# Reordering a list of twenty-five emission steps between an output projection and an up projection

## The chip, the cores and the metric

One core of a Trainium2 chip runs the whole program. The metric is the device time of one execution in microseconds (us); the median of several runs is compared.

## The reference

One layer of an encoder is applied to two batches, 512 and 256 positions (768 rows in all), 1024 channels, all in float32:

```
x = layernorm(x)
bg, cg, hc, q, k, v = split(x @ w_in)            # six blocks of 512 columns
y_conv = bg * dwconv3(cg * hc)                   # depthwise, three taps
y_attn = neighbourhood_attention(q, k, v, rpb)   # 8 heads of 64
y = concat(rmsnorm(y_conv), rmsnorm(y_attn))
x = layernorm(ALPHA * x + y @ w_o)               # the stage of this change
gate, val = split(dwconv3(x @ w_up))             # 1024 -> 2 * 2816
x = layernorm(ALPHA * x + (gelu(gate) * val) @ w_down)
```

## The kernel before, in words

The rows lie in six tiles of 128 positions, numbered 0 to 5. Tiles 2a and 2a+1 hold the even and the odd positions of a block of 256, so there are three blocks (a = 0, 1, 2). Every float32 matrix operand is split in a high part (a cast on ScalarE, line 99) and a low part (a subtraction on VectorE or GpSimd, line 100), and a product is three matmuls.

The up projection isn't done on even and odd positions one by one. It works on seven combinations ("roles" 1 to 7) of the even and odd operands and of the weights, so that seven products stand for eight. Buffer AR holds the seven combinations of x as operands: 0 and 1 are the two halves of the even tile, 2 comes from the odd tile alone, and 3, 4, 5, 6 are sums and differences of both. `OPS` (role to operand) is {1: 0, 2: 1, 3: 2, 4: 6, 5: 3, 6: 4, 7: 5}. So roles 1 and 2 need only even tiles; the others need the odd tile too.

The stage of this change stands between the attention half of the output projection (line 801) and the main loop of the up projection. Its pieces, by the letters of the list in the diff:

- `w`t is `wo_conv(t)`: 24 matmuls of 512 columns for tile t (line 822), in two halves; each half is added to the residual on VectorE (line 823). Then the norm of the tile: small VectorE sums (824, 209), a Square with a sum on ScalarE (210), a small VectorE operation (211), a power on GpSimd (212), a small VectorE product (826), and the scaling of the tile on ScalarE (827).
- `e`a is `x_even(a)`: eight TensorE transpositions of tile 2a (line 250), scaled out of PSUM by ScalarE (line 844), and then two operand splits (0 and 1).
- `o`a is `x_odd(a)`: the same for tile 2a+1, where VectorE scales one half (line 842), and then operands 2, 3, 5, 4, 6 in this order, with four VectorE sums or differences (lines 862, 864, 867, 869).
- `p`i prepares the weights of role i for the first pair of channel blocks (adds at lines 170 and 173, splits at 99 and 100).
- `a`i is `step(0, i, columns 0 to 255)`: the part of the first up product of role i that needs only blocks 0 and 1, 12 matmuls (line 180). After roles 1, 7 and 6 ScalarE copies the sum to another bank (lines 957, 963, 966), since a later role goes on from it; lines 943 and 949 fill parts of a bank that aren't summed yet.
- `l`c starts the loads of weights.

The rest of those roles (130 columns, block 2) and everything after is issued by the main loop, on TensorE in the order of the text. In the stage of the change only the transfers that SyncE starts (SP) are held to the order of the text (`tc.manual_schedule(engines={SP.engine})`). For the other engines a planner places the instructions ahead of time: the order of the text is their rank when several are ready by its own reckoning, and one that is ready earlier may stand earlier. The order on each engine is then fixed. The tiles `zt`, into which the transposed halves go, have seven buffers; PSUM has eight banks.

In this text "a1" means the 12 matmuls of `a1`, "tile 5's transpositions" the eight of `o2`, and so on; "piece i" is the 130-column rest of role i of the first pair. The steps that wait for each other around the change are these lines:

```python
V.scalar_tensor_tensor(o, q, ra[:, 0, t:t + 1], o, op0=OP.mult, op1=OP.add, accum_out=mv[:, n:n + 1])  # 823
A.activation(acc[t], acc[t], AF.Identity, bias=mv[:, 2:3], scale=mv[:, 3:4])                           # 827
q = transposed(bank("tr"), kn(acc[t])[:, 4 * c:4 * c + 4])                                             # x_tr
A.copy(role(c, 2)[:, n], role(c, 1)[:, n])                                                             # 957
```

Of the kernel before, what the change touches and what calls it, by code (L numbers as in the profile page):

```python
# [48 lines left out]
def encoder_kernel(ctx, tc, x, lnp, wv, wproj, wo_a, wo_c, wup, wdn, chan, rpb, mask, ident, out):  # L49
# [4 lines left out]
    def pool(name, **kw):  # L54
        g = tc.tile_pool(name=name, bufs=1, reuse_waits="tile", **kw)
        p = g.__enter__()
        return p, lambda: g.__exit__(None, None, None)
# [11 lines left out]
    def f(ap):  # L69
        return ap.bitcast(F32)  # L70
# [112 lines left out]
    a1, a1_close = pool("a1", side="right")  # L183
# [215 lines left out]
    a2, a2_close = pool("a2", side="right")  # L399
# [596 lines left out]
          "p": lambda i: pairs[0].prep(i), "a": lambda i: step(0, i, slice(0, Z0))}  # L996
    V.memset(f(AR[:, :, :, :, Z0:Z0 + 1]), 0.0)
    V.memset(f(AR[:, :, :, :, Z1:Z1 + 1]), 0.0)
    for z in "l0 l1 w0 p1 w1 e0 w2 o0 p7 w3 e1 p6 w4 o1 p2 w5 e2 p4 a1 a7 o2 a6 a2 a4 p5".split():
        EM[z[0]](int(z[1]))  # L1000
    lp_close()
    bp_close()
# [5 lines left out]
    for c in range(NC):  # L1008
        z = [(c, i) for i in (1, 7, 6, 2, 4, 5)]
# [233 lines left out]
```

## Time and profile before

| what | value |
|---|---|
| median of 3 runs | 864.44 us (864.15 to 867.42) |
| the profiled execution: its time, its span | 869.34 us, 867.6 us |
| TensorE busy, share of the span | 94% |
| VectorE busy | 79% |
| ScalarE busy | 57% |
| GpSimd busy | 26% |
| mean granted TensorE clock | 0.983 |

The span is the time from the first to the last instruction on the chip; the execution's own time is 1.74 us longer. The profiled execution was slower than the median of the runs by 4.9 us. Busy shares are averages over stages of different kinds.

### The profile page before, as it was taken

The numbers are of one execution on the slowest core, as the hardware profiler recorded it, in microseconds if no ns is written. First come the engines' busy times: TensorE is split into PE (matmuls) and PEld (weight loads), VectorE is DVE, ScalarE is ACT, GpSimd is POOL, SyncE is SP. The second block draws the span as 40 slices with busy tenths as digits, with TensorE's granted clock in tenths as the row PEclk, the third lists the DMA queues.
The fourth block names the chain that finished last, engine by engine and source line by source line (L and its number), as shares of the span: only waits on it lengthen the run. The fifth ranks groups of instructions, "written<-read, shape, count | busy, mean of one in ns | idle before, by whom it ended". The sixth has DMA issues, their size and how long they took to land.

```text
span 867.6 us, 13319 instructions
## 1 busy us (share of the span) xinstructions
PE 817.1 (94%) x4391; PEld 753.9 (87%) x4391; DVE 688.6 (79%) x1335; ACT 492.3 (57%) x1020; POOL 228.8 (26%) x286
## 2 busy tenths in 40 slices
PE   4899999979999999899999999999999889999995
PEld 3678999969898777899999999999999868888884
DVE  6997758867777667788888888888988699975675
ACT  4755656755676448765656555555556458445060
POOL 3555251354402431221433242232301000000101
PEclk9999999989999999899999999999999989999998
DMA  8688778776726750486998998899732399893361
GB/s 326 207 215 215 174 183 203 165 168 141 193 89 214 251 123 13 97 237 176 253 243 238 233 257 232 236 237 228 215 111 82 105 363 337 281 317 104 107 243 73
DMA packets 86421, 171.02 MB, mean 197 GB/s; under 512 B 12848, under 2 KB 26400, under 8 KB 86000
## 3 DMA queue, kind: packets, MB, share of 16 engines
q1 hardware_dynamic: 59552, 110.87, 39.5%
q0 software_dynamic: 25216, 54.74, 28.7%
q10 hardware_dynamic: 1584, 4.56, 1.3%
q8 instruction: 34, 0.56, 0.3%
q14 instruction: 35, 0.29, 0.1%
HBM read 142.70 MB, written 50.48 MB: 223 GB/s over the span
## 4 chain that ended last, share of the span: by engine, by line
PE 74%; DVE 10%; DMA 6%; ACT 5%; issue 3%; POOL 2%; SPq 0%; POOLq 0%; DVEq 0%; ACTq 0%
PE u L180 37%; PE dn L1061 19%; PE r L180 13%; DVE w L100 3%; DMA acc<-xa_d 2%; PE O L680 1%; PE S L623 1%; DVE AR L100 1%; ACT AR L99 1%; DMA vw<-v_d 1%; PE PT L656 1%; DMA br<-in_rpb 1%; DMA gb<-in_lnp 1%; DVE xr L233 1%; ACT sq L210 1%
## 5 line engine op out<-in xcount | busy, mean ns | idle before, releaser
L180 PE MATMUL u<-AR,w 128*128 128x386 f32 (+2 forms) x1908 | 333.5, 336 | 3.5 <-ACT u L957 3.5
L180 PEld LDWEIGHTS u<-AR,w 128*128 128x128 f32 x1908 | 332.2, 190 | 3.9 <-ACT u L957 3.8
L100 DVE TENSOR_TENSOR w<-raw,w 128x512 fp32r<-128x512 f32 x248 | 173.8, 713 | 59.2 <-ACT w L99 58.2
L99 ACT CAST w<-raw 128x512 fp32r<-128x512 f32 x255 | 156.4, 619 | 96.8 <-PE r L180 29.2
L1061 PE MATMUL dn<-w,hs 128*128 128x512 f32 (+1 forms) x714 | 163.6, 391 | 7.0 <-ACT hs L99 4.2
L1061 PEld LDWEIGHTS dn<-w,hs 128*128 128x128 f32 x714 | 132.4, 190 | 37.9 <-ACT hs L99 4.5
L180 PE MATMUL r<-AR,w 128*128 128x384 f32 x840 | 159.9, 342 | 2.4 <-ACT w L99 0.7
L180 PEld LDWEIGHTS r<-AR,w 128*128 128x128 f32 x840 | 146.9, 190 | 3.8 <-ACT w L99 1.0
L364 POOL DMA_DIRECT2D sw_d<-in_wdn x44 | 37.3, 929 | 106.3 <-DMA sw_d<-sw_d 82.5
L887 DVE SCALAR_TENSOR_TENSOR cu<-u,ch,cu 128x385 f32<-128x385 f32 (+1 forms) x88 | 52.1, 613 | 11.3 <-ACT cu L892 6.5
L99 ACT CAST hs<-hr 128x386 fp32r<-128x386 f32 x75 | 38.5, 514 | 36.9 <-DMA hr<-h_d 26.6
L100 DVE TENSOR_TENSOR w<-rw,w 128x512 fp32r<-128x512 f32 x70 | 47.1, 686 | 8.3 <-ACT w L99 8.3
L99 ACT CAST w<-rw 128x512 fp32r<-128x512 f32 x70 | 43.3, 621 | 15.8 <-issue 12.0
L887 DVE SCALAR_TENSOR_TENSOR cu<-cu,fwn 128x385 f32<-128x385 f32 (+1 forms) x88 | 48.5, 615 | 0.3 <-ACT cu L892 0.3
L909 POOL DMA_DIRECT2D h_d<-cu x33 | 24.2, 735 | 86.2 <-DVE cu L914 81.4
L1083 POOL TENSOR_TENSOR mv<-mv,expo 128x1 f32<-128x1 f32 x6 | 5.1, 854 | 157.9 <-DVE mv L1084 157.9
L100 DVE TENSOR_TENSOR hs<-hr,hs 128x386 fp32r<-128x386 f32 x75 | 41.0, 555 | 3.5 <-ACT hs L99 3.4
L801 PE MATMUL wo<-w,AR 128*128 128x512 f32 x144 | 34.5, 396 | 1.8 <-DVE acc L807 1.8
L822 PE MATMUL woc<-w,AR 128*128 128x512 f32 x144 | 34.7, 397 | 0.0
L801 PEld LDWEIGHTS wo<-w,AR 128*128 128x128 f32 x144 | 26.7, 188 | 8.5 <-DVE acc L807 2.6
L822 PEld LDWEIGHTS woc<-w,AR 128*128 128x128 f32 x144 | 26.8, 188 | 6.1
L303 PE MATMUL vp<-w,AR 128*128 128x512 f32 x108 | 29.2, 417 | 2.7 <-DVE AR L100 1.2
(193 smaller groups left out, 1078.8 us busy)
## 6 DMA issues: line engine op xcount, KB each, us to landing
raw<-in_wup SPq DMA_DIRECT2D x60, 256.0 KB, 6.5
hr<-h_d SPq DMA_DIRECT2D x75, 193.0 KB, 4.7
raw<-in_wproj SPq DMA_DIRECT2D x50, 256.0 KB, 5.4
rw<-in_wup SPq DMA_DIRECT2D x50, 256.0 KB, 6.8
sw_d<-in_wdn POOLq DMA_DIRECT2D x44, 256.0 KB, 9.5
raw<-sw_d SPq DMA_DIRECT2D x44, 256.0 KB, 4.7
raw<-in_wdn SPq DMA_DIRECT2D x33, 256.0 KB, 4.7
h_d<-ho POOLq DMA_DIRECT2D x11, 579.0 KB, 4.1
```

Of the source, the lines that this page charges most:

```text
L99: A.copy(hi, src)
L100: eng.tensor_sub(lo, src, f(hi))
L180: PE.matmul(q, w[:, g, k], AR[:, OPS[i], h, k, n], start=start and m == 0, stop=stop and m == 11, skip_group_check=True)
L210: A.activation(scratch, src, AF.Square, bias=mv[:, 0:1], accum_out=mv[:, 2:3])
L233: V.scalar_tensor_tensor(dst[n], dst[n], mv[:, 3:4], b[n], op0=OP.mult, op1=OP.add)
L303: PE.matmul(q, x_part(t, c)[:, h, k], wvo[4 * c + k][:, g], start=c + m + k == 0, stop=c == 1 and m == 2 and k == 3)
L364: return lambda: G.dma_start(sw_d[j, SW[i]], src, accum_op=OP.add)
L801: PE.matmul(banks[t], yas(h, i, t), wt[k][:, g], start=i == 0 and m == 0, stop=i == 3 and m == 2)
L822: PE.matmul(q, ycs(h, i, t), woc[i][n][:, g], start=i == 0 and m == 0, stop=i == 3 and m == 2)
L887: V.scalar_tensor_tensor(c[:, e, n], u[:, m], w, c[:, e, n], op0=OP.mult, op1=OP.add)
L909: G.dma_start(h_d[j, i:i + n].rearrange("o p n -> p o n"), src)
L1061: PE.matmul(q[:, x], hs[i, j][:, h, cols(a)], wd[i, j][:, g, x], start=i in (1, 7) and j == 0 and m == 0, stop=j == NJ - 1 and m == 2, ski ...
```

## The change

One string is changed: the order in which the steps of this stage are emitted. `w5` moves ahead of `o1` and `p2`; `a1` moves ahead of `e2` and `p4`; `o2` moves from behind `a7` to behind `a2`, ahead of `a4`. No instruction is added or removed.

```diff
     V.memset(f(AR[:, :, :, :, Z0:Z0 + 1]), 0.0)
     V.memset(f(AR[:, :, :, :, Z1:Z1 + 1]), 0.0)
-    for z in "l0 l1 w0 p1 w1 e0 w2 o0 p7 w3 e1 p6 w4 o1 p2 w5 e2 p4 a1 a7 o2 a6 a2 a4 p5".split():
+    for z in "l0 l1 w0 p1 w1 e0 w2 o0 p7 w3 e1 p6 w4 w5 o1 p2 a1 e2 p4 a7 a6 a2 o2 a4 p5".split():
         EM[z[0]](int(z[1]))
```

## Rows read from the trace of the kernel before

**Rows 1.** Page, part 1: busy us (share), instructions

```profile
PE 817.1 (94%) x4391; PEld 753.9 (87%) x4391; DVE 688.6 (79%) x1335; ACT 492.3 (57%) x1020; POOL 228.8 (26%) x286
```

**Rows 2.** Windows by stage: stretch, its length, busy us by engine, granted clock, DMA

```profile
307.50:366.00 58.50, 52.70 (x281) 44.72 (x279) 39.96 (x101) 40.67 (x81) 10.97 (x14) 0.94 0.32 72
366.00:450.00 84.00, 84.00 (x488) 84.00 (x489) 72.67 (x124) 50.97 (x90) 24.88 (x31) 1.00 0.81 218
...
690.00:720.00 30.00, 22.97 (x92) 18.11 (x91) 25.85 (x40) 16.98 (x33) 2.03 (x3) 0.89 0.94 332
```

**Rows 3.** TensorE in order of time: start, us, what [idle before, releaser]

```profile
341.21 1.09 PE L250 MATMUL tr<-idt,acc 128*128 128x128 f32 x8 [1.15 <-ACT acc L827]
342.06 5.83 PE L822 MATMUL woc<-w,AR 128*128 128x512 f32 x24
347.72 1.04 PE L250 MATMUL tr<-idt,acc 128*128 128x128 f32 x8
348.51 1.66 PE L180 MATMUL u<-AR,w 128*128 128x256 f32 x12
...
350.19 1.58 PE L180 MATMUL u<-AR,w 128*128 128x256 f32 x12
355.05 2.50 PE L180 MATMUL u<-AR,w 128*128 128x256 f32 x10 [3.28 <-ACT u L957]
357.35 1.91 PE L250 MATMUL tr<-idt,acc 128*128 128x128 f32 x8
...
359.80 6.00 PE L180 MATMUL u<-AR,w 128*128 128x256 f32 x48
366.00 8.54 PE L180 MATMUL u<-AR,w 128*128 128x130 f32 x60 [0.20 <-ACT u L957]
```

**Rows 4.** Windows of the stage, columns as in rows 2

```profile
341.00:342.00 1.00, 0.79 (x7) 0.79 (x8) 0.50 (x3) 1.00 (x3) 0.00 (x0) 1.00 0.00 0
...
352.00:354.00 2.00, 0.00 (x0) 0.00 (x0) 1.36 (x4) 2.00 (x5) 0.42 (x1) 0.93 0.34 131
...
355.00:356.00 1.00, 0.95 (x4) 0.95 (x5) 0.76 (x2) 0.63 (x1) 1.00 (x3) 0.50 0.00 0
...
360.00:362.00 2.00, 2.00 (x17) 2.00 (x16) 1.97 (x6) 1.58 (x3) 0.00 (x0) 0.86 0.92 166
```

**Rows 5.** ScalarE in order of time

```profile
344.49 1.25 ACT L827 ACTIVATE acc<-acc,mv 128x1024 f32<-128x1024 f32 x1
...
351.04 1.53 ACT L844 ACTIVATE zt<-tr,ch 128x128 f32<-128x128 f32 x4
352.42 0.66 ACT L99 CAST AR<-zt 128x512 fp32r<-128x512 f32 x1
352.93 1.19 ACT L210 ACTIVATE sq<-acc,mv 128x1024 f32<-128x1024 f32 x1
...
354.58 0.41 ACT L957 COPY u<-u 128x256 f32<-128x256 f32 x1
355.37 1.24 ACT L827 ACTIVATE acc<-acc,mv 128x1024 f32<-128x1024 f32 x1 [0.38 <-DVE mv L826]
```

**Rows 6.** VectorE in order of time

```profile
312.08 0.69 DVE L173 TENSOR_TENSOR raw<-raw 128x512 f32<-128x512 f32 x1
...
340.10 0.75 DVE L823 SCALAR_TENSOR_TENSOR acc<-woc,ra,acc 128x512 f32<-128x512 f32 x1 [0.28 <-PE woc L822]
...
349.13 0.69 DVE L100 TENSOR_TENSOR AR<-zt,AR 128x512 fp32r<-128x512 f32 x1
...
350.93 0.75 DVE L823 SCALAR_TENSOR_TENSOR acc<-woc,ra,acc 128x512 f32<-128x512 f32 x1
...
359.29 1.37 DVE L842 TENSOR_SCALAR zt<-tr,ch 128x128 f32<-128x128 f32 x4 [3.41 <-PE tr L250]
...
365.08 1.42 DVE L100 TENSOR_TENSOR AR<-zt,AR 128x512 fp32r<-128x512 f32 x2
```

**Rows 7.** GpSimd in order of time

```profile
351.24 1.18 POOL L100 TENSOR_TENSOR AR<-zt,AR 128x512 fp32r<-128x512 f32 x1 [7.03 <-ACT AR L99]
```

## The prediction

> **What bounds the kernel now.** I read the page first: TensorE is busy for 817.1 of 867.6 us [rows 1], so only what it loses can be won. The windows by stage show where. From 307.5 to 366 it is busy for 52.7 of 58.5 us at a mean clock of 0.94; from 366 to 450 it is busy for 84.00 of 84.00 [rows 2]. So in the up projection nothing but TensorE sets the time, and a microsecond won before 366 is carried on; its loss around 690 [rows 2] lies in the change to the down projection, which begins when the up products end, and moves along with them.
>
> TensorE in order of time shows what is lost near the change [rows 3]: 1.15 us before tile 3's transpositions, 3.28 us before a6, 0.20 us before piece 6. The 3.28 us cost more than themselves. The windows [rows 4] show the granted clock at 0.93 over 352 to 354, at 0.50 in 355 to 356, and at 0.86 over 360 to 362: it is at the lower level (1.2 instead of 2.4 GHz) from about 353.7 to 360.6, and TensorE works from 355.05 on, so 5.5 us of half clock lose 2.75 us. After the idle 1.15 us the clock stayed at 1.00 [rows 4]. Sum of what can be won: 1.15 + 3.28 + 2.75 + 0.20 = 7.4 us, 0.85% of the time.
>
> What made a6 wait is a ScalarE copy of a1's sum (line 957): a1's products ended near 350.2, and the copy ran at 354.58 [rows 3, 5]. ScalarE wasn't waiting in between: it did four scalings of e2, a cast, tile 5's Square, another cast, one behind the other [rows 5]. VectorE was as full: tile 5's second half sum ran at 350.93, though its products had ended at 347.9 [rows 3, 6]. The text has e2 and o1 ahead of these.
>
> **Does the text's order decide?** Not alone. An add for role 3's weights, which the text asks for in the main loop, runs at 312.08 [rows 6]; and ten of a6's matmuls stand ahead of tile 5's transpositions, though the text has them behind [rows 3]. So the order of the weights' preparation (p2, p4) doesn't matter: it was done early. Rank decides only where several are ready. The placement looks true to the chip's times: ten matmuls at full clock from 355.05 would end at 356.3, and the tile's scaling, which the transpositions need, ended at 355.37 + 1.24 = 356.6 [rows 3, 5]. I therefore place the new order by hand: on each engine the ready step of the highest rank, with the durations of the rows.
>
> **w5 ahead of o1.** Tile 4's products end at 341.21 - 1.15 = 340.06, and tile 5's follow at once instead of waiting for tile 3's transpositions. They take 5.83 us [rows 3] and end at 345.9, 2.0 us earlier. Tile 5's norm is then not behind o1's VectorE work: for tile 4, from its second half sum at 340.10 to the end of its scaling at 344.49 + 1.25, it took 5.6 us [rows 5, 6]. So tile 5 is ready for transposition at 345.9 + 0.1 + 5.6 = 351.6 instead of 356.6: 5 us. What pays is o1: tile 3's transpositions go from 341.21 to 345.9, 4.7 us later.
>
> **a1 ahead of e2.** Its operand comes from blocks' even tiles, and e1 is long done. After tile 3's transpositions (0.85 us from start to next start) come a1 (1.68 with what stands up to a7's start), then tile 4's transpositions (0.79), to 349.2 [rows 3]. The copy now ranks ahead of e2's scalings and runs near 349.6 instead of 354.58, so a2 and a6 no longer wait for it.
>
> **o2 behind a2, and what a7 waits for.** a7, a6 and a4 need o1's operands. Before, the last part of operand 5 was the split at 349.13, done 8.6 us after tile 3's transpositions began [rows 3, 6]; by this distance it is ready at 345.9 + 8.6 = 354.5, and with e2's ScalarE work moved behind o1's perhaps a microsecond sooner: 353.4 to 354.5, I take 354.0. Between 349.2 and 354.0 TensorE has a2 (even tiles only, 1.5 us, to 350.7) and tile 5's transpositions (ready at 351.6, to 352.45). Both are ready over a microsecond before a7, so I expect them ahead of it whatever the text says. That leaves idle pieces of 0.9 and 1.5 us, near the 1.15 us that left the clock up. Then a7, a6 and a4 (1.5 us each, 0.2 us for a filling; a4's operand is GpSimd's subtraction, which ended 11.2 us after tile 3's transpositions began [rows 3, 7], so 357.1) end at 358.7; pieces 1 and 7, at 1.5 us each (half of 359.80 to 365.80 [rows 3]), at 361.7. On TensorE alone piece 6 could start at 361.7 instead of 366.0: 4.3 us.
>
> Piece 6 also needs operand 4 of o2. ScalarE after 346.5 has, at starts 0.35 us apart for a scaling, 0.51 for a cast, 1.15 for a Square or the scaling of a tile [rows 5]: 16 scalings (o1 4, e2 8, o2 4: 5.6), 11 casts up to o2's operand 4 (o1 5, e2 2, o2 4: 5.6), one Square and one tile (2.3), three copies (1.1), together 14.6 us, to 361.1; VectorE's 0.7 us behind it makes 361.8. A second bound is the ring of seven `zt` buffers: o2's second half takes over a buffer of e1 that GpSimd's subtraction still reads, up to 357.1; from VectorE's first scaling of tile 5 to operand 4 took 359.29 to 365.7, so 6.4 us [rows 6], to 363.5. Between 361.8 and 363.5, and nearer to the latter, since some of ScalarE's waits will stay, I take 363.0 for piece 6.
>
> **The sum.** 366.0 - 363.0 = 3.0 us won. The bounds: 1.8 us, if o2 is another 1.2 us late, and 4.2 us, by ScalarE's sum. The profiled execution (869.34 us, span 867.6 and 1.74 around it) would become 866.3; it is 4.9 us above the median of the runs. Off the median, 864.44 - 3.0 = 861.4 us, 0.35% less. About 0.5% (4.3 us) is what a measurement of this kernel can tell from no change.
>
> **The rivals.**
>
> *A wait that takes the place of the old one, and the clock with it (slower).* If a2 and tile 5's transpositions stand behind a7 on TensorE, as the text has them, TensorE idles from 349.2 to 354.0, 4.8 us; the 3.28 us of before brought the clock down for 5.5 us of work [rows 3, 4]. a7, a6, a filling and a2 (4.7 us) then do 2.75 us of work by 359.5 and the rest by 361.45; tile 5's transpositions end near 362.3 instead of 359.27, and all behind them is 3.0 us later: 867.4 us. With a2 alone in the gap (3.3 us idle) it is 1.5 us later. It decides where a7 starts more than some 3 us after the work before it. Against it: tile 5 is ready some 2 us ahead of a7.
>
> The Trainium skill (TensorE: Matmul & The Clock Gate, HAM oscillation — how this bites in real kernels) has the rule behind this rival: a wait of TensorE long enough takes its clock to half, and the work behind the wait pays for it again. This trace agrees, with 3.28 us idle and 0.50 behind it [rows 3, 4].
>
> *All of the loss is won.* If o1's and o2's chains are shorter than the rows' distances, since their ScalarE work no longer meets e2's, TensorE never waits and piece 6 starts at 358.6 to 361.5: 4.4 to 7.4 us won, 859 us in the middle. Against it: ScalarE's 14.6 us from 346.5 hold only if it never waits for VectorE, and before it waited several times.
>
> *The change does little.* Ready times, not the text, place most of it; if o1's delay of 4.7 us eats tile 5's gain through the `zt` ring or through VectorE, the time stays within 1 us: 864 us.
>
> **Chances.** 3.0 us won (1.8 to 4.2): 0.58. All won: 0.12, most of it beyond 0.5%. Little: 0.16. Slower by 1 to 3 us: 0.11, within 0.5%. Something else, such as another placement of ScalarE's and VectorE's work in the first up products, to either side: 0.03. So faster by over 0.5% 0.14, within 0.5% 0.82, slower 0.04. The range leaves out the far half of the second case and the far part of the slower one: 859.4 to 866.0 us.
>
> **What the changed profile would show.** Right: no idle before tile 3's transpositions; 48 matmuls of line 822 in a row for tiles 4 and 5; the copy of line 957 just behind a1; a2 and tile 5's transpositions ahead of a7; no granted clock of 0.50 near 350 to 360; piece 6 near 363. Wrong: an idle stretch of 3 us or more before a7, with a low clock behind it; tile 5's transpositions behind a6 or a2; a new wait of piece 7 or 6 for o2's operands that gives back what was won; or another stretch of idle TensorE after 366.

## The result: slower by half a per cent, and the profile after

The changed kernel took 871.62 us (median of 18 runs, 867.11 to 878.79), the kernel before 866.1 us (18 runs, 862.73 to 874.91). The ratio is 1.0054 with a 95% interval of 1.0029 to 1.0080: by the ratio 4.7 us slower, where 3.0 us faster was forecast.

The profiled execution (872.84 us, span 871.0) reached the stage 4.2 us earlier than the one of before, through work that the change doesn't touch. So times of the stage are given from its first matmul of line 822, here after the change and before it:

```profile
303.53 11.34 PE L822 MATMUL woc<-w,AR 128*128 128x512 f32 x48
```

```profile
307.72 11.35 PE L822 MATMUL woc<-w,AR 128*128 128x512 f32 x48
```

The windows by stage of the changed kernel, with the columns of [rows 2]:

```profile
307.50:366.00 58.50, 52.88 (x276) 45.73 (x275) 37.42 (x98) 41.40 (x83) 10.02 (x13) 0.90 0.28 65
366.00:450.00 84.00, 84.00 (x463) 84.00 (x463) 68.07 (x116) 49.03 (x85) 23.40 (x30) 0.95 0.78 209
```

The busy time is almost that of before; the clock isn't: 0.90 instead of 0.94, and 0.95 instead of 1.00 in the stretch that had no loss at all. TensorE of the changed kernel in order of time:

```profile
329.92 11.43 PE L822 MATMUL woc<-w,AR 128*128 128x512 f32 x48
341.19 1.03 PE L250 MATMUL tr<-idt,acc 128*128 128x128 f32 x8
341.98 1.66 PE L180 MATMUL u<-AR,w 128*128 128x256 f32 x12
343.48 0.34 PE L943 MATMUL u<-w 128*128 128x386 f32 x1
343.67 1.03 PE L250 MATMUL tr<-idt,acc 128*128 128x128 f32 x8
347.74 0.58 PE L180 MATMUL u<-AR,w 128*128 128x256 f32 x1 [3.04 <-ACT AR L99]
348.12 0.52 PE L943 MATMUL u<-w 128*128 128x386 f32 x1
348.45 1.27 PE L250 MATMUL tr<-idt,acc 128*128 128x128 f32 x5
349.37 6.37 PE L180 MATMUL u<-AR,w 128*128 128x256 f32 x35
355.58 0.49 PE L250 MATMUL tr<-idt,acc 128*128 128x128 f32 x3
355.83 2.98 PE L180 MATMUL u<-AR,w 128*128 128x130 f32 x24
359.56 0.33 PE L180 MATMUL u<-AR,w 128*128 128x130 f32 x1 [0.76 <-ACT AR L99]
360.66 16.13 PE L180 MATMUL u<-AR,w 128*128 128x130 f32 x71 [0.77 <-DVE AR L100]
376.63 0.34 PE L943 MATMUL u<-w 128*128 128x386 f32 x1
```

A row merges matmuls of one line and shows the form of the first alone: the x71 at 360.66 are 47 matmuls of 130 columns, up to 370.75, and 24 of 386 columns (role 5, and role 1 of the second pair). The x60 of [rows 3] are 36 and 24 in the same way.

The 48 products stand in a row, and the 1.15 us of [rows 3] are gone. But one matmul of a7 (the x1 at 347.74) stands ahead of tile 5's transpositions, waits 3.04 us for the cast of its operand, and holds them up behind it; they are cut in five and three, the three behind a2. Later piece 7 waits twice, 0.76 and 0.77 us. The waits from the first product to the second pair add up to no more than before (0.88 + 0.17 + 3.04 + 0.76 + 0.77 = 5.6 us, against 5.8 by the same count before). What grew is the clock's part, as the windows of the changed kernel show:

```profile
350.00:352.00 2.00, 2.00 (x11) 2.00 (x11) 0.00 (x0) 2.00 (x6) 1.13 (x2) 0.50 0.00 0
...
354.00:355.00 1.00, 1.00 (x11) 1.00 (x10) 0.00 (x0) 0.65 (x3) 0.71 (x1) 1.00 0.99 152
...
362.00:364.00 2.00, 2.00 (x11) 2.00 (x11) 2.00 (x4) 1.32 (x3) 0.00 (x0) 0.50 0.00 0
...
372.00:374.00 2.00, 2.00 (x8) 2.00 (x7) 0.86 (x2) 1.31 (x2) 0.00 (x0) 0.50 0.07 13
374.00:376.00 2.00, 2.00 (x12) 2.00 (x12) 1.28 (x3) 0.62 (x1) 0.00 (x0) 0.93 0.32 118
```

After the long wait it is at 0.50, as before the change, and comes back. Then it falls a second time, at the 130-column pieces with piece 7's waits, and stays down for nearly 14 us (360.6 to 374.3), though TensorE is busy all the while from 360.66 on. The filling matmul (line 943) of the second pair closes the stage: 376.63 - 303.53 = 73.1 us, against 374.37 - 307.72 = 66.65 in the profile of before.

### The profile page after: what moved, and what is told of

The parts are those of the page before. It is cut to its first block, busy times and chain, and to the rows that moved or that the text cites. A ratio compares the mean times of both kernels' runs of the same rounds, so it can differ in the third digit from the quotient of the medians.

```text
span 871.0 us, 13320 instructions
## 1 busy us (share of the span) xinstructions
PE 822.6 (94%) x4391; PEld 758.7 (87%) x4391; DVE 686.3 (79%) x1335; ACT 491.8 (56%) x1020; POOL 229.3 (26%) x286
## 4 chain that ended last, share of the span: by engine, by line
PE 72%; DVE 9%; DMA 8%; issue 4%; ACT 4%; POOL 1%; SPq 1%; POOLq 0%; ACTq 0%; DVEq 0%
PE u L180 38%; PE dn L1061 15%; PE r L180 10%; DVE w L100 2%; PE vp L303 2%; DMA raw<-in_wproj 2%; PE woc L822 1%; DMA acc<-xa_d 1%; DMA raw<-sw_d 1%; PE O L680 1%; PE tr L250 1%; DMA vw<-v_d 1%; PE S L623 1%; PE PT L656 1%; DMA raw<-in_wv 1%
## 5 line engine op out<-in xcount | busy, mean ns | idle before, releaser
L180 PE MATMUL u<-AR,w 128*128 128x386 f32 (+2 forms) x1908 | 340.5, 341 | 4.6 <-ACT AR L99 3.8
L180 PEld LDWEIGHTS u<-AR,w 128*128 128x128 f32 x1908 | 338.8, 194 | 5.2 <-ACT AR L99 4.2
```

The lines of the kernel that those rows point to most:

```text
L180: PE.matmul(q, w[:, g, k], AR[:, OPS[i], h, k, n], start=start and m == 0, stop=stop and m == 11, skip_group_check=True)
```

## The experiments

The theories. **A:** the cost lies in the granted clock, set off by waits. **B:** it lies in tile 5's late operands; the clock only goes along. **C**, formed after four runs: moving a1 ahead of e2 costs, whatever else is done. **D:** the narrow pieces bring the clock down, waits or not. **E**, after eight runs: an order only decides where TensorE waits for tile 5, and a wait at the pieces costs most, through the clock. **F:** falls come by chance. Ratios are to the kernel before, run in the same rounds on the same chip, with a 95% interval. Where one line of an order is shown, it is the new one; lines left out of an edit are marked by dots.

**1. w5 alone.**

```diff
-    for z in "l0 l1 w0 p1 w1 e0 w2 o0 p7 w3 e1 p6 w4 o1 p2 w5 e2 p4 a1 a7 o2 a6 a2 a4 p5".split():
+    for z in "l0 l1 w0 p1 w1 e0 w2 o0 p7 w3 e1 p6 w4 w5 o1 p2 e2 p4 a1 a7 o2 a6 a2 a4 p5".split():
```

> Only w5 is moved ahead of o1 and p2; a1 and o2 stay where they were before the change. Theory A (what the change costs is TensorE's lower granted clock, set off by its waits, not the sum of the waits): a7 has to wait about 3 us for tile 3's late operand and a6 then waits again for the copy of a1, which still ranks behind e2; the clock is at 0.50 for 6 us or more behind that, and the time is 0.2 to 0.8% above the kernel before. Theory B (what costs is that tile 5's operands come late, because its transpositions are cut in five and three; the clock is a by-product): tile 5's transpositions stand whole and ahead of most of a7 here, so its operands come 2 us earlier than with the whole change, and the time is that of before or up to 0.3% less.

Measured: 0.9975 (0.9942 to 1.0008). TensorE of it:

```profile
357.02 0.58 PE L180 MATMUL u<-AR,w 128*128 128x256 f32 x1 [3.06 <-ACT AR L99]
357.40 1.91 PE L250 MATMUL tr<-idt,acc 128*128 128x128 f32 x8
358.96 2.69 PE L180 MATMUL u<-AR,w 128*128 128x256 f32 x11
361.45 0.53 PE L943 MATMUL u<-w 128*128 128x386 f32 x1
362.19 16.06 PE L180 MATMUL u<-AR,w 128*128 128x256 f32 x120 [0.22 <-ACT u L957]
378.09 0.34 PE L943 MATMUL u<-w 128*128 128x386 f32 x1
```

A's forecast of a loss failed, B's held. The long wait is there as in the whole change, and the clock was down behind it; but it came back at about 363, and from 362.19 on there are 120 matmuls without a wait of 0.15 us or more, the pieces among them, through which the clock stays up:

```profile
366.00:368.00 2.00, 2.00 (x20) 2.00 (x19) 2.00 (x4) 0.42 (x1) 0.00 (x0) 1.00 0.99 176
```

So not every fall costs the same.

**2. a1 alone.**

```diff
+    for z in "l0 l1 w0 p1 w1 e0 w2 o0 p7 w3 e1 p6 w4 o1 p2 w5 a1 e2 p4 a7 o2 a6 a2 a4 p5".split():
```

> Only a1 is moved ahead of e2 and p4; w5 stays behind o1, and o2 behind a7. Theory A: tile 3's operands come as early as before, and the copy of a1 runs two scalings earlier on ScalarE, so the wait of 3.28 us before a6 falls under 1.5 us, the clock stays at 1.00, and the time is 0.3 to 0.6% under the kernel before (3 to 5 us). Theory B: tile 5's transpositions stand behind a2, as late as before, so its operands set the end as before, and the time is within 0.15% of before.

Measured: 1.0056 (1.0023 to 1.0089). Both fail. The wait ahead of a6 fell to 0.86 us and the clock stayed up until the pieces, as A said; but TensorE then ran into tile 5's late operands there:

```profile
365.30 1.68 PE L180 MATMUL u<-AR,w 128*128 128x130 f32 x12 [0.77 <-DVE AR L100]
367.71 14.28 PE L180 MATMUL u<-AR,w 128*128 128x130 f32 x59 [0.73 <-DVE AR L100]
```

Fifty-nine matmuls in 14.28 us, where sixty took 8.54 us before [rows 3]: half clock (0.50 from 366.7 to 380.3), in a profile with no wait above 1.13 us.

```profile
370.00:372.00 2.00, 2.00 (x11) 2.00 (x11) 0.69 (x1) 0.79 (x2) 0.00 (x0) 0.50 0.38 131
```

This execution took 877.74 us, and its mean granted clock, 0.976, is the lowest of the eleven runs that the ratio goes by; what the others show of the clock stands under "The clock" below.

**3. A filler in the long wait of the whole change.** Sixteen matmuls keep TensorE busy ahead of a7.

```diff
+    def fill(q, count):
+        w = pairs[0].w[7][:, 0]
+        for _ in range(count):
+            PE.matmul(q, w[:, 0:P], w[:, 0:HT], start=True, stop=True, skip_group_check=True)
...
         elif i == 7:
+            if c == 0 and n.start == 0:
+                fill(role(0, 4), 16)
             k.prod(7, role(c, 4)[:, n], n.start == 0, True, n)
```

> The whole change, with 16 matmuls of 386 columns (about 2.9 us at full clock) into the bank that a7 is going to overwrite, ahead of a7, where TensorE waits 3.04 us. They do no useful work; the result is the same. Theory A: TensorE has no idle stretch there, the clock stays at 1.00 until piece 7, and the time is 3 to 9 us (0.35 to 1%) under that of the whole change, so between 0.995 and 1.002 of the kernel before. Theory B: the operands come no earlier, so the time is that of the whole change, 1.003 to 1.008 of the kernel before, or worse by the filler.

Measured: 1.0036 (1.0007 to 1.0065). The clock stayed up ahead of the pieces, as A said; but piece 7 still waited 0.78 and 0.77 us, and the clock fell there. The ratio lies in B's range and above A's, though the interval reaches into A's. That some of the whole change's loss (1.0054) came back isn't shown: the intervals overlap.

**4. A filler in the wait of the kernel before** (the same `fill`, into `role(0, 3)`, 18 matmuls behind a7).

> The kernel before, with 18 such matmuls behind a7, where TensorE waits 3.28 us for the copy of a1; they go into a bank that is overwritten later, and the result is the same. Theory A: the clock stays at 1.00, and of the 2.75 us that the half clock lost most comes back: 0.995 to 0.998 of the kernel before. Theory B: the wait is full of other work but ends when it did, and the operands of tile 5 set the end: 0.999 to 1.003.

Measured: 1.0026 (1.0003 to 1.0050). That is in B's range and not in A's: taking the long wait's idle time away made the kernel slower, if by little (the interval ends just above 1). TensorE, and the windows behind:

```profile
364.24 13.33 PE L180 MATMUL u<-AR,w 128*128 128x130 f32 x60 [0.70 <-ACT u L962]
```

```profile
362.00:364.00 2.00, 1.54 (x14) 1.40 (x12) 1.97 (x4) 1.22 (x3) 0.00 (x0) 1.00 0.04 8
...
370.00:372.00 2.00, 2.00 (x10) 2.00 (x10) 1.27 (x3) 1.24 (x4) 0.87 (x1) 0.50 0.32 81
```

What counts here is 0.70 us of waiting, the longest since tile 3's transpositions, and a half clock for some ten microseconds behind it (364.6 to 374.8). The wait is by the profile for ScalarE's copy of piece 1 (line 957 before, which the inserted lines move to 962), not for tile 5's operands. The fillers also move the planned order (tile 5's transpositions behind 8 matmuls of a6 instead of 10).

**5. o2 put back** into the whole change.

```diff
+    for z in "l0 l1 w0 p1 w1 e0 w2 o0 p7 w3 e1 p6 w4 w5 o1 p2 a1 e2 p4 a7 o2 a6 a2 a4 p5".split():
```

> The whole change except for o2, which goes back to its place behind a7. In the planned order one matmul of a7 still stands ahead of tile 5's transpositions, but these are whole instead of cut in five and three. Theory A, as the first four runs have changed it (the cost lies in the granted clock, and above all in a second fall at the 130-column pieces, which a short wait of piece 7 just ahead of them brings about and which lasts until the 386-column products): tile 5's last operands come about 3 us earlier than in the whole change, piece 7 hardly waits, and the time is 0.994 to 1.000 of before, as with w5 alone. Theory C (the cost lies in moving a1 ahead of e2, which cost 0.56% by itself, however o2 stands): 1.003 to 1.007 of before.

Measured: 1.0028 (0.9994 to 1.0063), between the two forecasts and nearer to C's. Tile 5's operands came 3.0 us earlier than in the whole change (its last subtraction ended 57.7 us after the first product, not 60.7), yet TensorE reached the pieces earlier too, waited 0.44 and 0.82 us there, and the clock fell.

**6. Both waits of the whole change filled** (as 3, and nine matmuls ahead of piece 7).

```diff
+            if c == 0 and n.start:
+                fill(role(1, 1), 9)
             k.prod(7, role(c, 4)[:, n], n.start == 0, True, n)
```

> The whole change with the 16 filling matmuls ahead of a7 as in the third run, and 9 more of 386 columns (1.6 us at full clock) ahead of piece 7, into a bank that the next pair's first product overwrites. The result is the same. Theory A: TensorE is hardly idle ahead of the pieces, the clock stays at 1.00 through them, and of the 6 to 7 us that the half clock took there most come back: 0.995 to 0.999 of before, against 1.0036 with the first filler alone. Rival D (the narrow pieces bring the clock down by themselves, waits or not): no better than the first filler alone, 1.002 to 1.007.

Measured: 1.0021 (0.9995 to 1.0048), in D's range; A expected more. The profile, though, shows no fall at all, with 0.19 and 0.82 us of waits left, and the shortest stage but one (65.6 us). So the narrow pieces don't bring the clock down by themselves, as D had it; before the change they hadn't either. This execution was the shortest of its twelve; number 16 takes this up.

**7. Piece 7 made late in the kernel before.**

```diff
+        for _ in range(4 if a == 2 else 0):
+            V.tensor_scalar(ol, ol, 1.0, None, op0=OP.mult)
         V.tensor_sub(ol, oh, ol)
         x_op(ol, 5, a, es[1])
```

> The kernel before, with four multiplications by 1 of 128x512 on VectorE (about 0.35 us each) in tile 5's chain ahead of operand 5, so that piece 7 has to wait 1 to 2.5 us, just ahead of the pieces; the result is the same. Theory A: the clock falls at the pieces in most executions, and the time is 3 to 7 us (0.35 to 0.8%) above before, well over the delay itself. Theory B (what counts is how late the operands are): 1 to 2.5 us above before, 0.1 to 0.3%.

Measured: 1.0098 (1.0061 to 1.0134), about 8.5 us for waits of 3.28 and 0.62 us (the planner also put operands 4 and 6 ahead of 5, so the wait is longer than meant):

```profile
365.35 0.48 PE L180 MATMUL u<-AR,w 128*128 128x130 f32 x1 [3.28 <-ACT AR L99]
366.45 16.49 PE L180 MATMUL u<-AR,w 128*128 128x130 f32 x71 [0.62 <-DVE AR L100]
```

The time behind the wait, 71 matmuls in 16.49 us, is that of the whole change. A wait at the pieces cost over twice its own length; B, which counts the wait alone, fails, and even A's 0.35 to 0.8% is exceeded.

**8. Half of w5 ahead of o1**, the other half behind it (`f5` and `g5` are the two halves of `wo_conv(5)`).

```diff
+    for z in "l0 l1 w0 p1 w1 e0 w2 o0 p7 w3 e1 p6 w4 f5 o1 p2 g5 a1 e2 p4 a2 o2 a7 a6 a4 p5".split():
```

> A new order: only the first half of tile 5's products stands ahead of o1, the second half behind it; then a1, tile 4's transpositions, a7, a2, tile 5's transpositions, a6, a4. So tile 3's transpositions don't wait, its operands are 1.8 us later than before instead of 4.7, and a1's copy no longer stands behind all of e2. Theory A: no wait of TensorE above 1.5 us up to a6, and tile 5's operands 1 to 2 us earlier than before; 0.993 to 0.998 of before if the clock stays up at the pieces, 1.000 to 1.004 if tile 5's transpositions, now behind a2, come so late that piece 7 waits. Theory C (a1 ahead of e2 costs by itself): 1.003 or more.

Measured: 1.0016 (0.9986 to 1.0046). a2 stood ahead of all the rest and waited for a1's copy (line 957, here moved to 962):

```profile
356.47 2.93 PE L180 MATMUL u<-AR,w 128*128 128x256 f32 x12 [5.39 <-ACT u L962]
```

The longest wait of all, three 256-column steps ahead of the pieces, cost little: the clock was back at the pieces. Both forecasts are missed: A's 0.993 to 0.998 for a clock that stays up there, and C's 1.003 or more, which the interval still takes in.

**9. o2 alone.**

```diff
+    for z in "l0 l1 w0 p1 w1 e0 w2 o0 p7 w3 e1 p6 w4 o1 p2 w5 e2 p4 a1 a7 a6 a2 o2 a4 p5".split():
```

> Only o2 is moved, behind a2; w5 and a1 stay as before the change. Reading E (so far: in every order ScalarE and VectorE finish tile 5's operands 57 to 61 us after the first product of the stage, and an order only decides where TensorE waits for them; a wait just ahead of the 130-column pieces costs most, because the clock then stays at 0.50 until the 386-column products): a6 waits 3.3 us as before, tile 5's transpositions stand behind a6 and a2 and start some 2 us later, its last operand comes at 60 us or later instead of 58.8, piece 7 waits about 2 us, the clock falls again at the pieces, and the time is 0.4 to 1.0% above before. Theory C (moving a1 ahead of e2 is what costs): within 0.2% of before.

Measured: 1.0079 (1.0046 to 1.0112), with a1 where it was: moving a1 isn't the cause of all, and E held. Piece 7 waited 0.77 and 0.77 us, and the clock fell behind.

**10. The whole change with o2 ahead of a7.**

```diff
+    for z in "l0 l1 w0 p1 w1 e0 w2 o0 p7 w3 e1 p6 w4 w5 o1 p2 a1 e2 p4 o2 a7 a6 a2 a4 p5".split():
```

> The whole change, but with o2 ahead of a7 instead of behind a2, so that tile 5's transpositions don't queue behind the one matmul of a7, and ScalarE scales tile 5 ahead of the copies of a7 and a6. Reading E: tile 5's last operand comes 2 to 4 us earlier than in the whole change (57 to 58.5 us after the first product), piece 7 waits under 1 us, and the time is 0.996 to 1.001 of before. Theory C: 1.003 to 1.007, as the other orders with a1 ahead of e2.

Measured: 1.0038 (1.0004 to 1.0071). The forecast from E missed, and C's (1.003 to 1.007) was met: tile 5's last operand came at 58.3 us, as E expected, but TensorE, waiting less ahead, was at the pieces sooner (piece 1 at 49.5 us from the first product, not 52.3) and waited 0.62, 0.20, 0.77 and 0.82 us there. To bring the operands forward is no use when TensorE comes forward as much. In all seven orders and fillings that have a1 ahead of e2 the ratio lies above 1, so C isn't refuted as a rule of thumb; number 9 shows only that other moves cost too.

**11. w5 ahead of o1, o2 ahead of a1, and 12. w5 ahead of o1, o2 between a1 and a7.**

```diff
+    for z in "l0 l1 w0 p1 w1 e0 w2 o0 p7 w3 e1 p6 w4 w5 o1 p2 e2 p4 o2 a1 a7 a6 a2 a4 p5".split():
```

```diff
+    for z in "l0 l1 w0 p1 w1 e0 w2 o0 p7 w3 e1 p6 w4 w5 o1 p2 e2 p4 a1 o2 a7 a6 a2 a4 p5".split():
```

> w5 ahead of o1 as in the change, and o2 directly behind e2, ahead of a1. Reading E: all of tile 5's operands are ranked ahead of the first sums, so they come early (54 to 57 us after the first product); TensorE's long wait comes ahead of a6, for the copy of a1, 4.5 us of 256-column work before the pieces, and nothing waits at the pieces: 0.993 to 0.998 of before. If the wait ahead of a6 grows past 4 us, 0.998 to 1.002.

> w5 ahead of o1 as in the change, a1 behind e2 as before, and o2 ahead of a7. It differs from w5 alone (0.9975) only in tile 5's transpositions no longer standing behind one matmul of a7. Reading E: tile 5 is transposed 1 to 2 us earlier, nothing waits at the pieces, the wait ahead of a7 or a6 stays 3 us: 0.994 to 0.998 of before.

Measured: 0.9981 (0.9948 to 1.0014) and 0.9981 (0.9952 to 1.0010). Both wait ahead of the pieces (3.47 us ahead of tile 5's transpositions; 1.88 us there and 1.75 us ahead of a6) and not at them, and the ratios lie at the upper end of E's ranges, a hair outside. E's way to it was in part wrong: in number 11 tile 5's last operand came at 58.3 us and not at 54 to 57. With number 1 they are the best orders tried, but none is faster than the kernel before by more than its interval.

**13 to 16. More profiles** of the kernel before (two), of the whole change, and of number 6.

> The kernel before, once more, for its profile alone. Reading E: TensorE doesn't wait over 0.5 us ahead of the pieces, and the clock stays at 1.00 through them; the stage, from its first product to the first filling of the second pair, takes 65 to 67 us. Rival F (the clock falls at the pieces by chance, whether TensorE waits there or not, and the single profiles so far were luck): a fall at the pieces with no wait of over 0.5 us ahead of it, and a stage of 69 us or more.

> The same once more: reading E expects no fall at the pieces without a wait ahead of them, rival F expects one in about half of the profiles.

> The changed kernel, once more, for its profile alone. Reading E: piece 7 waits 1 to 2 us, the clock falls there and stays at 0.50 for 10 us or more, and the stage takes 69 to 74 us. Rival F: the same wait with the clock at 1.00 about as often as not, and a stage of 65 to 67 us.

> The whole change with both fillers (16 matmuls ahead of a7, 9 ahead of piece 7), once more: its profile showed no fall at all although 1.0 us of waits was left ahead of the pieces, but its median was 1.0021 of before. Reading E: in other executions the rest of the waits brings the fall at the pieces, so this profile may show it (stage 69 us or more). Rival F: the profile shows a fall elsewhere, or none.

Measured, one execution each: 863.41, 864.79, 868.46 and 870.96 us. TensorE at the pieces, in the first of before, the whole change and number 6 again:

```profile
358.77 8.54 PE L180 MATMUL u<-AR,w 128*128 128x130 f32 x60 [0.48 <-ACT u L957]
367.15 0.34 PE L943 MATMUL u<-w 128*128 128x386 f32 x1
```

```profile
347.20 0.39 PE L180 MATMUL u<-AR,w 128*128 128x256 f32 x1 [3.05 <-ACT AR L99]
...
360.03 12.85 PE L180 MATMUL u<-AR,w 128*128 128x130 f32 x59 [0.82 <-DVE AR L100]
372.72 0.34 PE L943 MATMUL u<-w 128*128 128x386 f32 x1
```

```profile
361.88 13.19 PE L180 MATMUL u<-AR,w 128*128 128x130 f32 x59 [0.82 <-DVE AR L100]
374.91 0.34 PE L943 MATMUL u<-w 128*128 128x386 f32 x1
```

The windows at the pieces, of before and of the whole change:

```profile
360.00:362.00 2.00, 2.00 (x20) 2.00 (x19) 1.91 (x3) 1.02 (x3) 0.00 (x0) 1.00 0.00 0
```

```profile
362.00:364.00 2.00, 2.00 (x11) 2.00 (x11) 0.51 (x1) 0.79 (x2) 0.00 (x0) 0.50 0.37 131
```

Neither profile of before has a fall at the pieces, as E expected; the second waited 0.70 us there in one piece, over E's bound, and kept its clock. The whole change fell there again, this time without a fall after its wait of 3.05 us. Number 6 now fell too, with the same waits at which it hadn't: chance (F) has a part where the waits are short.

All profiles of the stage, from the first product to the filling of the second pair (the waits are those of 0.15 us or more; 0.16 in number 8, 0.62 in 10 and 0.63 in 2 are a4's, which stands among the pieces there):

| kernel | from, to | us | waits from piece 1 on | clock at the pieces | ratio |
|---|---|---|---|---|---|
| before | 307.72, 374.37 | 66.65 | 0.20 | 1.00 | |
| before (13) | 300.97, 367.15 | 66.18 | 0.48 | 1.00 | |
| before (14) | 303.46, 369.32 | 65.86 | 0.70 | 1.00 | |
| 1 w5 alone | 312.79, 378.09 | 65.30 | none | 1.00 | 0.9975 |
| 11 | 303.06, 369.58 | 66.52 | none | 1.00 | 0.9981 |
| 12 | 305.69, 371.59 | 65.90 | none | 1.00 | 0.9981 |
| 8 half of w5 | 309.86, 376.31 | 66.45 | 0.16 | 1.00 | 1.0016 |
| 6 both fillers | 304.55, 370.16 | 65.61 | 0.19 + 0.82 | 1.00 | 1.0021 |
| 6 again (16) | 304.94, 374.91 | 69.97 | 0.17 + 0.82 | falls | |
| 4 filler, before | 307.57, 377.41 | 69.84 | 0.70 | falls | 1.0026 |
| 5 o2 back | 309.82, 379.35 | 69.53 | 0.44 + 0.82 | falls | 1.0028 |
| 3 filler | 306.23, 376.67 | 70.44 | 0.78 + 0.77 | falls | 1.0036 |
| 10 | 311.27, 381.47 | 70.20 | 0.62 + 0.20 + 0.77 + 0.82 | falls | 1.0038 |
| whole change | 303.53, 376.63 | 73.10 | 0.76 + 0.77 | falls | 1.0054 |
| whole change (15) | 302.80, 372.72 | 69.92 | 0.70 + 0.77 + 0.82 | falls | |
| 2 a1 alone | 309.89, 381.83 | 71.94 | 0.25 + 0.63 + 0.19 + 0.77 + 0.73 | falls | 1.0056 |
| 9 o2 alone | 303.39, 376.52 | 73.13 | 0.77 + 0.77 | falls | 1.0079 |
| 7 late piece 7 | 306.73, 382.79 | 76.06 | 3.28 + 0.62 | falls | 1.0098 |

Where the clock stays up at the pieces, the stage takes 65.3 to 66.7 us, whatever the order; where it falls, 69.5 us or more. The ratios follow the waits at the pieces only roughly: 1.5 us of them stand beside 1.0036, 1.0054 and 1.0079. All eight profiles with 1.26 us or more there show a fall; of the four with 0.70 to 1.01 us two do.

## Why the prediction was wrong

**What held.** TensorE in fact sets the time, and nothing behind the stage gave anything back (494.4 us in the profile of after, 493.2 before). Tile 5's products ended at 341.35, 37.8 us after the first product instead of 40.2. Tile 5's norm ended at 345.27 + 1.24 = 346.5, 43.0 us after it, where 351.6 - 307.72 = 43.9 was forecast. The placement by rank and readiness came out this far; it failed at the two places that follow.

**a1's copy.** It was to run near 349.6 (41.9 us after the first product), so that a2 could stand in the wait ahead of a7. It ran 44.6 us after. ScalarE of the changed kernel:

```profile
345.27 1.24 ACT L827 ACTIVATE acc<-acc,mv 128x1024 f32<-128x1024 f32 x1 [0.30 <-DVE mv L826]
346.42 1.82 ACT L99 CAST AR<-zt 128x512 fp32r<-128x512 f32 x3
348.14 0.37 ACT L957 COPY u<-u 128x256 f32<-128x256 f32 x1
...
352.74 0.41 ACT L963 COPY raw<-u 128x256 f32<-128x256 f32 x1
354.35 0.36 ACT L966 COPY u<-u 128x256 f32<-128x256 f32 x1 [1.21 <-PE u L180]
354.62 1.51 ACT L844 ACTIVATE zt<-tr,ch 128x128 f32<-128x128 f32 x4
```

I had put the copy ahead of e2's scalings and forgotten that o1's casts, which rank above it, were still to come: three of them stand ahead, behind tile 5's scaling.

**"Both are ready over a microsecond before a7, so I expect them ahead of it."** This is the step of the placement that failed. a2 wasn't ready, for the reason above. Tile 5 was ready at 346.5, as forecast; but a7 doesn't need its whole operand to begin. Its first matmul needs the high part only, a cast, and the plan put this one matmul ahead of the transpositions. So a wait of 3.04 us took the place of the old 3.28 us, and tile 5's transpositions stood behind it.

**Piece 6 at 363.0, 3.0 us won.** This is the term that was mis-sized. Tile 5's last subtraction ended at 363.53 + 0.68, 60.7 us after the first product, where before it was 58.8. VectorE of the changed kernel:

```profile
356.11 1.36 DVE L842 TENSOR_SCALAR zt<-tr,ch 128x128 f32<-128x128 f32 x4 [2.39 <-PE tr L250]
...
363.53 0.68 DVE L100 TENSOR_TENSOR AR<-zt,AR 128x512 fp32r<-128x512 f32 x1
```

ScalarE's sum of 14.6 us assumed that ScalarE never waits for TensorE. It does: tile 5's scalings (354.62) stand behind the copies of a7 and a6, the second of which waited 1.21 us for products at half clock; and VectorE waited 2.39 us for the three transpositions that stand behind a2. In the profile in which the clock stayed up until the pieces (number 15), piece 6 was past its last wait at 360.03 - 302.80 = 57.2 us; before, at 57.5 (number 14), 57.8 (13) and 58.3. So the reordering won 0.3 to 1.1 us there instead of 3.0, and even this flatters it: all three profiles of before have a fall ahead of the pieces, which number 15 happened not to have.

**The clock.** The prediction had the fall as a rival, priced only ahead of a7 (3.0 us), and took from one row that waits up to 1.15 us leave the clock up. That row stood among 512-column products. At the pieces, waits of 0.70 to 0.82 us came with a fall in ten of the twelve profiles that had one there or longer, and it lasted 10 us or more. From piece 6 to the filling of the second pair it took 367.15 - 358.77 = 8.4 us at full clock (number 13) and 372.72 - 360.03 = 12.7 us in the whole change (number 15): 4.3 us lost against 0.6 won gives the stage's 69.92 - 66.18 = 3.7 us. Where the clock falls after the long wait as well, it was 6 to 7 us. The measured 4.7 us lies between. The closing paragraph of the prediction names this very case ("a new wait of piece 7 or 6 for o2's operands that gives back what was won"), but no chance and no price had been given to it, and the range ended at 866.0. Its own figures held the case: TensorE alone could start piece 6 at 361.7, the operands let it start at 363.0, and those 1.3 us of waiting at the pieces were put at no cost to the clock. This is the term that turned the sign; the whole change waited 1.53 us there.

The granted clock of all runs, and not only of the profiled ones, is a rough check, since it counts idle stretches too. The share of the clock that was lost, times the span, comes on average to 16.2 us in the whole change and to 13.1 us before (in the rounds of numbers 1 to 4): 3.1 of the 4.9 us between their mean times. It is 4.7 of 6.0 us in number 9 and 6.0 of 7.8 us in number 7, but only 1.0 of 4.2 us in number 2. So the clock is the larger part of the whole change's loss; the rest of it, and most of what a1 alone costs, the runs don't explain.

**Which part cost.** o2 alone cost 0.79%, a1 alone 0.56%, and w5 alone nothing (0.9975). The first makes tile 5 late; the second takes away the wait ahead of a6, so that TensorE is at the pieces before tile 5. The parts don't add up: all three together cost 0.54%. What stays open is what decides a fall when only 0.7 to 1.0 us are waited: the same program fell in one execution and not in another (numbers 6 and 16).

## What to carry to other kernels

When two engines behind TensorE set when its last operands come, moving work about only chooses where TensorE waits; here a wait ahead of the 256-column sums cost less than one at the 130-column pieces, where the clock's fall cost more than the wait. That the width is the reason isn't shown: no run moved the same wait to wider products at the same place. Taking an early wait away can move it to the worse place: compute where the saved time meets the next late operand before counting it as won. And when reading an order, ask what the first instruction of a step needs, not the step as a whole: one matmul that is ready in the plan and not on the chip holds up everything behind it.

## What the runs showed of the hardware that was not expected

The clock went to half in or just behind stretches with waits of 0.70 to 0.82 us among 130-column matmuls and stayed there for 10 to 17 us with TensorE at work nearly all the while, whereas 1.15 us among 512-column products left it at 1.00, and a wait of 3.05 us (number 15) was followed by no fall where the same program had fallen after 3.04 us. In all ten profiles with a fall at the pieces it came back 1.9 to 5.1 us after the 386-column products had begun; a fall ahead of the pieces lasted 3 to 7 us. The same program fell at the pieces in one execution and not in the other, with the same waits (numbers 6 and 16). Filling an idle stretch with useless matmuls, so that the clock stayed up there, made the kernel before slower by 0.26% (0.03 to 0.50%).
